# The up projection of a gated feed-forward: high and low activation parts as one 512-column operand

## The chip, the core and the metric

The kernel runs on one core of a Trainium2 chip. Its time is the device time of one execution in microseconds (us), from runs on the chip. TensorE multiplies matrices into PSUM, eight banks of 128 partitions by 512 float32 values; VectorE (DVE), ScalarE (ACT) and GpSimd (POOL) do elementwise work; SyncE (SP) issues the loads of the weights. A profile is one execution taken by the hardware's profiler. In its rows PE is TensorE's matmul, PEld its weight load (the load of the stationary operand, which lies beside the matmul before it).

## The reference, cut to what matters

One decoder layer over 256 tokens of width 2048 in float32. The change lies in the feed-forward part only:

```
def _conv_ffn(h, w_up, conv_w, conv_b, w_down):
    a = h @ w_up                      # (256, 2048) @ (2048, 11264)
    a = depthwise causal convolution of width 3 over the tokens (a) + conv_b
    gate, val = jnp.split(a, 2, axis=-1)
    return (jax.nn.silu(gate) * val) @ w_down
```

The input h of this part is a RMS norm of the residual. Its scale by token is put on after the product, since a product with w_up commutes with it.

## The kernel before

Float32 precision is reached with operands split in two parts of the shorter type float32r: a high part (the value rounded) and a low part (what the rounding lost). A product is three matmuls: high weights by high activations, high weights by low activations, low weights by high activations. The helper `mm3` issues them: for each of 8 row tiles the first two, one behind the other with the same stationary weight tile, and then 8 of the third kind.

The weights come as a stream of chunks of 128 partitions by 1024 values, eight 128x128 tiles each. SP loads a chunk into a `raw` tile (L120), ACT rounds it to `hi` (L150) and DVE takes the difference to `lo` (L151). `w_next` hands out the next split chunk and has the two after it prepared. The pool `wp` has three tiles each of `hi` and `lo`, so a split waits until the chunk three before it has been used by its last matmul.

The up projection is a loop of 44 iterations. Each makes 128 gate channels and 128 value channels for all 256 tokens, out of four chunks: gate first and second half of the 2048 inputs, then value first and second half. Weights are stationary (128x128), activations move (128x256). The activations `x2h` and `x2l` stay in SBUF for the whole loop. Gate and value share one PSUM bank (`mm`, of three), 256 columns each. When both are done, DVE multiplies the bank by the scale by token, `r2`, into `abuf` (L1069); ACT and DVE make the convolution (tile `cv`, L1075 to L1079), ACT the SiLU (L1082), POOL the product (L1083), ACT and POOL the two parts of the result, `hid` (L1084, L1085).

Behind the loop comes the down projection (L1122), with `hid` stationary and `w_down` moving, 512 columns wide: a chunk there is 12 matmuls. At its start DVE transposes the residual `hT` into tiles `ht` (L1100) and ACT issues 16 loads that bring them to `ho` (L1102). These take the place of the activations of the up projection (tags `xh0` to `xh3` and `rA`).

Elsewhere in the kernel one more product has 512 moving columns: the values of the attention (`v_chunk`, L855 to L857), with the latents `chl` stationary and split weights moving.

The order on each engine is set by a scheduler ahead of time; each engine then runs its queue strictly in that order, and waits where an instruction needs another engine's result.

Of the kernel before, what the change touches and what calls it, by code (L numbers as in the profile page):

```python
# [20 lines left out]
# How many steps of the state space follow each chunk of weights until its output is needed: the chunks  # L21
# of u, of the latents, of keys, values and queries, the last heads, the attention half of the output.
# [15 lines left out]
# Column layout of the packed per-partition parameters.  # L38
# [16 lines left out]
def layer_kernel(ctx: ExitStack, tc: tile.TileContext, pack, pos, xt, bk, w_in, w_kpe, w_uqn,  # L55
# [17 lines left out]
    # every chunk: 128 partitions x up to 1024 values, split exactly into two float32r parts  # L73
# [53 lines left out]
    def load_after(dst, src):  # L127
        """A load that stays behind the weights asked for so far."""
        with tc.issue_after(state["last"]):
            SP.dma_start(dst, src)  # L130

    def w_prep_to(n):
        while state["prep"] < min(n, len(chunks)):
# [3 lines left out]
            if i == KPE_AT + 1:  # L137
                # the rotary key is a float32 product with the input rows as they are: its weights take the norm's
# [23 lines left out]
    def mm3(ps, wh, wl, xh, xl, nk, first, last):  # L162
        """ps += sum over k of w[k].T @ x[k], each operand given as two parts."""
# [5 lines left out]

    def col(t, k, n=128):  # L170
        return t[:, k * n:(k + 1) * n]

# [8 lines left out]
    def quads(dtype, name):  # L181
        """Sixteen row tiles, four to a tile."""
# [15 lines left out]
    # the first half of the input rows and of three column tiles arrive two row tiles at a time  # L198
# [27 lines left out]
    # a few products of ones bring the array to its full clock before the data is there  # L226
# [19 lines left out]
    def tok_sums(parts, ps=None):  # L246
        """Sums over partitions and parts, token t of the half h in column h of a PSUM tile."""
# [7 lines left out]
    def tok_rsqrt(ps, n, eps=None):  # L255
        """1 / sqrt(ps / n + eps) by token."""
# [5 lines left out]
    def tok_rows(r):  # L262
        """The values by token as a row, alike in every partition."""
# [6 lines left out]
    def row_scale(dst, parts, n, eps=None):  # L270
        """dst[p, t] = 1 / sqrt(sum over partitions and parts / n + eps), alike in every row."""
        r = tok_rsqrt(tok_sums(parts), n, eps)
        A.copy(dst, tok_rows(r))
        return r

    def split_scaled(hi, lo, src, w):
        """hi + lo = src * w (one value of w per partition), hi in float32r."""
# [26 lines left out]
    def wrap(dst, src, k):  # L304
        """dst = src less the nearest multiple of 2 pi."""
# [14 lines left out]
    # factors of the complex products, the second set for the imaginary part of the other operand  # L320
# [6 lines left out]
    def ssm_setup():  # L327
# [21 lines left out]
        # columns: powers 0..4 of the state layout, then the key layout, each step with its own power  # L349
# [9 lines left out]
        # phase of a chunk of four steps in turns, and in two parts of which one has few bits  # L359
# [24 lines left out]
        # z = (abar - 1) / lambda  # L384
# [18 lines left out]
        # z times the powers, pair index outermost: [re | -im] and [-im | -re]  # L403
# [23 lines left out]
    # cos and sin of i * phi for the 64 chunks, eight pairs at a time  # L427
# [28 lines left out]
    # matrices of the state space, four pairs of groups at a time  # L456
# [8 lines left out]
    def ssm_in_products(b):  # L465
        """Chunk inputs to states times abar, laid [(step, p32), ...]: the two halves of the complex products."""
# [18 lines left out]
    def ssm_out_mats(b, c):  # L485
        """States (times abar) to outputs: C z abar^l, real (c = 0) and negated imaginary part."""
# [40 lines left out]
    def ssm_k(b):  # L527
        """Lag matrices: values of input b against C z abar^l."""
# [11 lines left out]
    def ssm_m(b):  # L540
        """Within a chunk: lag matrices placed by step, the skip on the diagonal."""
# [731 lines left out]
```

## Time and profile before

| | |
|---|---|
| median of 3 runs | 1113.42 us (1112.39 to 1113.47) |
| profiled execution, from first to last instruction | 1111.5 us |
| TensorE busy in it | 1066.4 us, 96% |
| DVE busy | 736.2 us, 66% |
| ACT busy | 611.0 us, 55% |
| POOL busy | 286.0 us, 26% |
| up projection, first to last matmul | 350.4 to 858.2 us |
| mean granted clock of TensorE | 0.991 of 2.4 GHz |

The span of the profiled execution stands 1.9 us below the median of the runs; the rows give no other time of that execution. Busy shares count an engine as busy for the whole modelled duration of its instructions, and matmuls overlap in a pipeline, so the time that one more matmul costs is read from the distance between starts.

### The profile page before, as it was taken

Reading aid. Unit: us, or ns where it says so; the run is one execution under the profiler, and the core shown is the slowest. Engines: PE = TensorE matmul, PEld = TensorE weight load, DVE = VectorE, ACT = ScalarE, POOL = GpSimd, SP = SyncE. Lnnn points to the kernel's source line nnn. Section 1 sums busy time; section 2 is a strip of 40 time slices with the busy share of each in tenths; the row PEclk is TensorE's granted clock in tenths of the full one; section 3 lists DMA queues with packets and bytes.
Section 4 is the critical chain, followed back from the end, with each engine's and each line's share of the span. In section 5 each row is a group of like instructions: output and inputs, shape, how many; then the busy total and the mean of one; then the engine's idle time right before and its main releaser. Section 6 shows DMA issues by size and latency. Waiting matters only on the chain.

```text
span 1111.5 us, 20545 instructions
## 1 busy us (share of the span) xinstructions
PE 1066.4 (96%) x8264; PEld 1002.9 (90%) x8264; DVE 736.2 (66%) x998; ACT 611.0 (55%) x986; POOL 286.0 (26%) x284
## 2 busy tenths in 40 slices
PE   7979899787999999999999999999999999999997
PEld 7979877786999999999999999999999888888896
DVE  8999898797798665656566565665657545454543
ACT  6567578857765645555555455555554434343433
POOL 7371745773333121211212112121211000000000
PEclk9989999999999999999999999999999999999999
DMA  6635341433555455555555555555555965555652
GB/s 211 227 115 172 134 130 61 171 134 131 173 176 186 172 189 189 174 188 180 182 189 183 180 189 174 188 189 180 182 182 185 258 227 189 189 189 189 210 190 76
DMA packets 56672, 195.40 MB, mean 176 GB/s; under 512 B 6528, under 2 KB 8448, under 8 KB 56576
## 3 DMA queue, kind: packets, MB, share of 16 engines
q1 hardware_dynamic: 54576, 190.93, 50.0%
q10 hardware_dynamic: 2000, 3.16, 1.1%
q8 instruction: 65, 1.06, 0.4%
q14 instruction: 31, 0.25, 0.1%
HBM read 189.86 MB, written 2.10 MB: 173 GB/s over the span
## 4 chain that ended last, share of the span: by engine, by line
PE 78%; DVE 11%; ACT 5%; issue 3%; DMA 3%; POOL 0%; SPq 0%; ACTq 0%; DVEq 0%
PE mm L168 18%; PE mm L166 18%; PE mm L165 18%; PE mm L1122 11%; PE wk L1122 11%; DVE lo L151 3%; ACT yT L610 1%; DMA bkt<-in_bk_dram 1%; DVE epad L477 1%; PE wk L913 1%; DVE hT L992 1%; PE wk L912 1%; ACT u L512 1%; DMA raw<-in_w_in_dram 1%; DVE sh L578 1%
## 5 line engine op out<-in xcount | busy, mean ns | idle before, releaser
L151 DVE TENSOR_TENSOR lo<-raw,hi 128x1024 fp32r<-128x1024 f32 x329 | 411.4, 1252 | 256.0 <-ACT hi L150 253.5
L150 ACT CAST hi<-raw 128x1024 fp32r<-128x1024 f32 x329 | 343.4, 1047 | 305.8 <-PE mm L166 113.2
L166 PE MATMUL mm<-x2l,hi 128*128 128x256 f32 x1408 | 345.6, 283 | 0.0
L165 PE MATMUL mm<-x2h,hi 128*128 128x256 f32 x1408 | 345.6, 283 | 0.0
L165 PEld LDWEIGHTS mm<-x2h,hi 128*128 128x128 f32 x1408 | 270.3, 192 | 0.0
L166 PEld LDWEIGHTS mm<-x2l,hi 128*128 128x128 f32 x1408 | 270.3, 192 | 0.0
L168 PE MATMUL mm<-x2h,lo 128*128 128x256 f32 x1408 | 197.6, 283 | 0.0
L168 PEld LDWEIGHTS mm<-x2h,lo 128*128 128x128 f32 x1408 | 181.6, 192 | 0.0
L1083 POOL TENSOR_TENSOR cv<-cv 128x256 f32<-128x256 f32 x44 | 68.0, 1545 | 389.4 <-ACT cv L1082 375.8
L1122 PE MATMUL wk<-hi,hid 128*128 128x512 f32 (+1 forms) x360 | 88.1, 364 | 0.0
L1122 PE MATMUL mm<-hi,hid 128*128 128x512 f32 x312 | 85.4, 395 | 0.0
L1122 PEld LDWEIGHTS wk<-hi,hid 128*128 128x128 f32 x360 | 63.5, 188 | 13.0
L1069 DVE TENSOR_TENSOR abuf<-mm,r 128x512 f32<-128x512 f32 x43 | 29.7, 691 | 62.2 <-PE mm L168 62.2
L1122 PEld LDWEIGHTS mm<-hi,hid 128*128 128x128 f32 x312 | 57.8, 188 | 13.1
L1075 ACT ACTIVATE cv<-abuf,pk 128x256 f32<-128x256 f32 x88 | 48.3, 595 | 28.5 <-DVE abuf L1069 26.9
L1084 ACT CAST hid<-cv 128x256 fp32r<-128x256 f32 x44 | 17.9, 406 | 75.1 <-POOL cv L1083 71.8
L1122 PE MATMUL wk<-lo,hid 128*128 128x512 f32 (+1 forms) x180 | 50.9, 364 | 0.0
L165 PE MATMUL mm<-xh,hi 128*128 128x256 f32 x184 | 48.0, 294 | 2.5 <-ACT hi L150 2.5
L1122 PE MATMUL mm<-lo,hid 128*128 128x512 f32 x156 | 49.0, 395 | 0.0
L166 PE MATMUL mm<-xl,hi 128*128 128x256 f32 x184 | 47.6, 292 | 0.0
L493 POOL TENSOR_TENSOR m<-bkt,pp 128x256 f32<-128x256 f32 x32 | 30.2, 955 | 61.2 <-DMA bkt<-in_bk_dram 47.2
L610 ACT ACTIVATE yT<-wk 32x64 f32<-32x64 f32 x128 | 35.6, 278 | 7.8 <-PE wk L604 6.3
(330 smaller groups left out, 1641.4 us busy)
## 6 DMA issues: line engine op xcount, KB each, us to landing
raw<-in_w_up_dram SPq DMA_DIRECT2D x176, 512.0 KB, 3.2
raw<-in_w_down_dram SPq DMA_DIRECT2D x88, 512.0 KB, 4.2
raw<-in_w_out_dram SPq DMA_DIRECT2D x32, 512.0 KB, 3.3
raw<-in_w_in_dram SPq DMA_DIRECT2D x25, 512.0 KB, 3.3
bkt<-in_bk_dram SPq DMA_DIRECT2D x8, 512.0 KB, 5.6
raw<-in_w_glu_dram SPq DMA_DIRECT2D x8, 512.0 KB, 3.3
raw<-in_w_uqn_dram SPq DMA_DIRECT2D x4, 512.0 KB, 4.3
hT<-in_xt_dram SPq DMA_DIRECT2D x4, 512.0 KB, 4.9
```

What stands on the lines that cost most here:

```text
L150: A.copy(hi, raw)
L151: V.tensor_tensor(out=lo, in0=raw, in1=hi.bitcast(F32), op=ALU.subtract)
L165: PE.matmul(ps, wh(k), xh(k), start=(first and k == 0), stop=False)
L166: PE.matmul(ps, wh(k), xl(k), start=False, stop=False)
L168: PE.matmul(ps, wl(k), xh(k), start=False, stop=(last and k == nk - 1))
L493: G_.tensor_tensor(out=m, in0=ci[:, s].unsqueeze(2).to_broadcast([P, 4, 4, 16]), in1=pp[:, s, c].rearrange("p (q l) -> p q l", l=4)[:, cb, ...
L610: A.activation(dst[:, j], psy[32 * j:32 * j + 32, q], AF.Gelu_apprx_tanh)
L1069: V.tensor_tensor(out=a[:, :, 2:T + 2], in0=ps, in1=r2.unsqueeze(1).to_broadcast([P, 2, T]), op=ALU.mult)
L1075: A.activation(t, a[:, gv, 2:T + 2], AF.Identity, bias=prm("conv_b", ch_, 1), scale=prm("conv_w", 176 + ch_, 1))
L1083: G_.tensor_tensor(out=cv[0], in0=cv[0], in1=cv[1], op=ALU.mult)
L1084: A.copy(hid[0][:, i, :], cv[0])
L1122: PE.matmul(ps[:, 0:n], hid[x][:, 2 * i + k, ts_], w[wk][:, 512 * k + c0:512 * k + c0 + n], start=(i == 0 and s == 0 and k == 0), stop=(i ...
```

## The change

The activations' two parts are laid side by side, `x2(k)` of 2 x 256 columns (tiles `x2a` for the first eight row tiles, `x2b` for the others). A new helper `mm_wide` sends both as one moving operand of 512 columns behind each high weight tile, and the 256 columns of the high part behind each low weight tile. Products with the high activations land in the first half of a bank, products with the low activations and with the low weights in the second half. So gate and value take a bank each, one of the pool `mm` and one of `wk`. On the way out ACT copies the second half to SBUF (`low`), DVE adds the first half to it into `abuf`, and the multiplication by `r2` follows from SBUF to SBUF. Nothing else differs but comments and the numbers of lines (+9 or +10 in this part).

```diff
+    def mm_wide(ps, wh, wl, xp, nk, first, last):
+        n = ps.shape[-1] // 2
+        for k in range(nk):
+            PE.matmul(ps, wh(k), xp(k), start=(first and k == 0), stop=False)
+        for k in range(nk):
+            PE.matmul(ps[:, n:], wl(k), xp(k)[:, 0], start=False, stop=(last and k == nk - 1))
...
-    x2h = r0.tile([P, 16, T], F32R, tag="rA", name="x2h")
-    x2l = quads(F32R, "x2l")
+    x2a = [r0.tile([P, 2, 2, T], F32R, tag=f"xh{i}", name=f"x2{i}") for i in range(4)]
+    x2b = r0.tile([P, 8, 2, T], F32R, tag="rA", name="x2b")
+
+    def x2(k):
+        return x2a[k // 2][:, k % 2] if k < 8 else x2b[:, k - 8]
...
-        split_scaled(x2h[:, ct, :], x2l(ct), hT[:, ct, :], prm("ffn_norm", ct, 1))
+        split_scaled(x2(ct)[:, 0], x2(ct)[:, 1], hT[:, ct, :], prm("ffn_norm", ct, 1))
...
     for i in range(44):
-        if i == 0:
-            pgv = [mm_bank()[:, :T], mm_bank()[:, :T]]
-        else:
-            ps = mm_bank().rearrange("p (a t) -> p a t", a=2)
-            pgv = [ps[:, 0], ps[:, 1]]
+        pgv = [mm_bank(), wk_bank()]
+        a = abuf[i % 2]
         for gv, hf in up_order(i):
             wh, wl = w_next()
-            mm3(pgv[gv], lambda k: col(wh, k), lambda k: col(wl, k),
-                lambda k: x2h[:, 8 * hf + k, :], lambda k: x2l(8 * hf + k), 8, hf == 0, hf == 1)
+            mm_wide(pgv[gv], lambda k: col(wh, k), lambda k: col(wl, k), lambda k: x2(8 * hf + k), 8,
+                    hf == 0, hf == 1)
+            if hf == 1:
+                t = fp.tile([P, T], F32, tag=f"cv{gv}", name="low")
+                A.copy(t, pgv[gv][:, T:])
+                V.tensor_tensor(out=a[:, gv, 2:T + 2], in0=pgv[gv][:, 0:T], in1=t, op=ALU.add)
         if i == 0:
             row_scale(r2, [hacc], D)
-        a = abuf[i % 2]
-        if i == 0:
-            for gv in range(2):
-                V.tensor_tensor(out=a[:, gv, 2:T + 2], in0=pgv[gv], in1=r2, op=ALU.mult)
-        else:
-            V.tensor_tensor(out=a[:, :, 2:T + 2], in0=ps, in1=r2.unsqueeze(1).to_broadcast([P, 2, T]),
-                            op=ALU.mult)
+        V.tensor_tensor(out=a[:, :, 2:T + 2], in0=a[:, :, 2:T + 2], in1=r2.unsqueeze(1).to_broadcast([P, 2, T]),
+                        op=ALU.mult)
```

Where this moves instructions is seen in the order of the built programs, which holds no time. First TensorE's queue, one chunk (second half of a gate) in the middle of the up projection before; a wait names the engine whose counter it watches, and of the eight pairs the first four stand here:

```order
L165 MATMUL mm<-x2h,hi 128x256 [waits Activation_49]
L166 MATMUL mm<-x2l_3725,hi 128x256
L165 MATMUL mm<-x2h,hi 128x256
L166 MATMUL mm<-x2l_3725,hi 128x256
L165 MATMUL mm<-x2h,hi 128x256
L166 MATMUL mm<-x2l_3725,hi 128x256
L165 MATMUL mm<-x2h,hi 128x256
L166 MATMUL mm<-x2l_3725,hi 128x256
```

The same chunk with the change, whole:

```order
L175 MATMUL mm<-x2b,hi 128x512 [waits Activation_49]
L175 MATMUL mm<-x2b,hi 128x512 x7
L177 MATMUL mm<-x2b,lo 128x256 [waits DVE_49]
L177 MATMUL mm<-x2b,lo 128x256 x7
```

A chunk goes from 16 + 8 matmuls of 256 columns to 8 of 512 and 8 of 256. Up to the loop, TensorE's queue is the same in both programs.

Second, ACT's queue in one iteration in the middle of the loop, before (`cv` from `abuf` is the convolution's first term, `hid` the rounded result; DMAHW names the lanes on which loads report):

```order
L150 CAST hi<-raw 128x1024 [waits DMAHW0_49,DVE_49,PE_49]
L1075 ACTIVATE cv<-abuf_4346,pk 128x256 [waits DVE_49]
L1075 ACTIVATE cv<-abuf_4346,pk 128x256
L150 CAST hi<-raw 128x1024 [waits DMAHW1_49,PE_49,Activation_49]
L1082 ACTIVATE cv<-cv 128x256 [waits DVE_49]
L1084 CAST hid_4343<-cv 128x256 [waits Pool_49]
L150 CAST hi<-raw 128x1024 [waits DMAHW2_49,PE_49,Activation_49]
L150 CAST hi<-raw 128x1024 [waits DMAHW3_49,PE_49,Activation_49]
```

And with the change:

```order
L1075 COPY low<-mm 128x256 [waits PE_49,Pool_49]
L1092 ACTIVATE cv<-cv 128x256 [waits DVE_49]
L1094 CAST hid_4343<-cv 128x256 [waits Pool_49]
L150 CAST hi<-raw 128x1024 [waits DMAHW7_49,PE_49,Activation_49]
L150 CAST hi<-raw 128x1024 [waits DMAHW0_49,PE_49,Activation_49]
L1075 COPY low<-wk 128x256 [waits PE_49]
L150 CAST hi<-raw 128x1024 [waits DMAHW1_49,DVE_49,PE_49]
L1085 ACTIVATE cv<-abuf_4346,pk 128x256 [waits DVE_49,Activation_49]
L1085 ACTIVATE cv<-abuf_4346,pk 128x256
L150 CAST hi<-raw 128x1024 [waits DMAHW2_49,PE_49,Activation_49]
```

Two copies have come in, each waiting for TensorE to finish an accumulation, and the SiLU of an iteration now stands behind the copy of the next iteration's gate. The four roundings of weights (L150) stand between them; counted from the start of the loop, the first behind the hid cast belongs to the chunk that TensorE starts three chunks after the gate has ended.

Third, ACT's queue a little behind the loop, where the last loads of `ho` stand between the roundings of the seventh and the eighth chunk of `w_down`, before:

```order
L150 CAST hi<-raw 128x1024 [waits DMAHW5_49,PE_49,Activation_49]
L1102 DMA ho<-ht_10414 32x2x512 [waits DMAHW5_49]
L1090 ACT_TABLE_LOAD
L1090 ACTIVATE warm<-hid_4344,eps_t 128x1 [waits Pool_49]
L1102 DMA ho<-ht_10414 32x2x512 [waits DMAHW6_49]
L1102 DMA ho<-ht_10414 32x2x512 [waits DMAHW7_49]
L1102 DMA ho<-ht_10414 32x2x512 [waits DMAHW1_49]
L150 CAST hi<-raw 128x1024 [waits DVE_49,PE_49] x3
```

And with the change:

```order
L150 CAST hi<-raw 128x1024 [waits PE_49,Activation_49]
L1112 DMA ho<-ht_9312 32x2x512 [waits DMAHW4_49]
L1094 CAST hid_4343<-cv 128x256 [waits Pool_49]
L1112 DMA ho<-ht_9312 32x2x512 [waits DMAHW6_49]
L1112 DMA ho<-ht_9312 32x2x512 [waits DMAHW7_49]
L1100 ACT_TABLE_LOAD
L1100 ACTIVATE warm<-hid_4344,eps_t 128x1 [waits Pool_49]
L1112 DMA ho<-ht_9312 32x2x512 [waits DMAHW1_49]
L150 CAST hi<-raw 128x1024 [waits PE_49,Activation_49]
```

The last `hid` cast has slipped in among the loads, and the loads wait for other lanes; the rounding of the eighth chunk still stands behind the sixteenth load.

## Rows read from the trace of the kernel before

**Rows 1.** The page: busy time by engine, and the chain that ended last.

```profile
PE 1066.4 (96%) x8264; PEld 1002.9 (90%) x8264; DVE 736.2 (66%) x998; ACT 611.0 (55%) x986; POOL 286.0 (26%) x284
PE 78%; DVE 11%; ACT 5%; issue 3%; DMA 3%; POOL 0%; SPq 0%; ACTq 0%; DVEq 0%
PE mm L168 18%; PE mm L166 18%; PE mm L165 18%; PE mm L1122 11%; PE wk L1122 11%; DVE lo L151 3%; ACT yT L610 1%; DMA bkt<-in_bk_dram 1%; DVE epad L477 1%; PE wk L913 1%; DVE hT L992 1%; PE wk L912 1%; ACT u L512 1%; DMA raw<-in_w_in_dram 1%; DVE sh L578 1%
```

**Rows 2.** Windows of 50 us: PE, PEld, DVE, ACT, POOL busy, granted clock, DMA.

```profile
500.00:550.00 50.00, 50.00 (x419) 50.00 (x418) 30.71 (x41) 26.92 (x36) 9.32 (x8) 1.00 0.52 180
600.00:650.00 50.00, 50.00 (x419) 50.00 (x419) 30.39 (x38) 25.11 (x33) 9.04 (x8) 1.00 0.52 184
```

**Rows 3.** Instructions of L165 and L168: durations in ns, first and last start in us.

```profile
L165 PE MATMUL mm<-x2h,hi x1408: 279/283/362, 350.4 to 857.0; 128*128 128x256 f32 x176
...
L168 PE MATMUL mm<-x2h,lo x1408: 281/283/283, 352.3 to 858.0; 128*128 128x256 f32 x176
```

**Rows 4.** Timeline of PE in the up projection: start, us, instruction.

```profile
600.77 0.28 PE L166 MATMUL mm<-x2l,hi 128*128 128x256 f32 x1
600.89 1.12 PE L168 MATMUL mm<-x2h,lo 128*128 128x256 f32 x8
601.85 0.28 PE L165 MATMUL mm<-x2h,hi 128*128 128x256 f32 x1
601.97 0.28 PE L166 MATMUL mm<-x2l,hi 128*128 128x256 f32 x1
...
603.77 1.12 PE L168 MATMUL mm<-x2h,lo 128*128 128x256 f32 x8
604.73 0.28 PE L165 MATMUL mm<-x2h,hi 128*128 128x256 f32 x1
```

**Rows 5.** The chain in order of time, in the down projection: six 512-column matmuls a piece.

```profile
978.73 1.40 PE mm L1122 x6
```

**Rows 6.** Timeline of PE at the first chunk of attention values (512 columns).

```profile
155.07 0.40 PE L855 MATMUL mm<-hi,chl 128*128 128x512 f32 x1
...
155.54 0.39 PE L857 MATMUL mm<-lo,chl 128*128 128x512 f32 x1
...
156.46 0.39 PE L855 MATMUL mm<-hi,chl 128*128 128x512 f32 x1
...
156.91 0.39 PE L857 MATMUL mm<-lo,chl 128*128 128x512 f32 x1
...
157.59 0.39 PE L857 MATMUL mm<-lo,chl 128*128 128x512 f32 x1
```

**Rows 7.** Timeline of PE in the last quarter of the down projection: 256 columns.

```profile
1089.97 1.53 PE L1122 MATMUL wk<-xw,hid 128*128 128x256 f32 x12
1091.33 1.09 PE L1122 MATMUL mm<-hi,hid 128*128 128x512 f32 x4
```

**Rows 8.** Groups by line and form: count, busy us, mean ns, idle before.

```profile
L273 ACT COPY r<-wk 128x256 f32<-128x256 f32 x1 | 0.4, 372 | 1.2 <-PE wk L266 1.2
L1067 DVE TENSOR_TENSOR abuf<-mm,r 128x256 f32<-128x256 f32 x2 | 0.8, 420 | 0.3 <-ACT r L273 0.3
L1132 DVE TENSOR_TENSOR ho<-ho,fw 128x512 f32<-128x512 f32 x6 | 3.9, 684 | 0.0
L1069 DVE TENSOR_TENSOR abuf<-mm,r 128x512 f32<-128x512 f32 x43 | 29.7, 691 | 62.2 <-PE mm L168 62.2
```

**Rows 9.** Timeline of ACT over one iteration: start, us, idle before and its releaser.

```profile
651.73 1.10 ACT L1075 ACTIVATE cv<-abuf,pk 128x256 f32<-128x256 f32 x2 [0.64 <-DVE abuf L1069]
652.97 1.05 ACT L150 CAST hi<-raw 128x1024 fp32r<-128x1024 f32 x1
654.05 0.42 ACT L1082 ACTIVATE cv<-cv 128x256 f32<-128x256 f32 x1
656.18 0.41 ACT L1084 CAST hid<-cv 128x256 fp32r<-128x256 f32 x1 [1.71 <-POOL cv L1083]
656.49 1.04 ACT L150 CAST hi<-raw 128x1024 fp32r<-128x1024 f32 x1
```

**Rows 10.** Timeline behind the loop: PE's start of the down projection; ACT and PE at its eighth chunk.

```profile
858.16 1.10 PE L1122 MATMUL mm<-hi,hid 128*128 128x512 f32 x4
...
875.54 0.59 ACTq L1102 DMA_DIRECT2D ho<-ht  x1
...
876.23 2.95 ACT L150 CAST hi<-raw 128x1024 fp32r<-128x1024 f32 x3 [2.14 <-DMA raw<-in_w_down_dram]
...
877.77 1.10 PE L1122 MATMUL mm<-hi,hid 128*128 128x512 f32 x4
```

## Prediction

> **What bounds the kernel now.** I read the page first. TensorE is busy for 96% of the span, and 78% of the chain that ended last is its work; the three lines of `mm3` alone (L165, L166, L168) hold 18% each [rows 1]. A busy share of an engine whose matmuls overlap proves little, so the second view is the windows. In the up projection TensorE shows no hole in 50 us, at the full clock (granted share 1.00, the 2.4 GHz level), with DVE at 30.4 to 30.7 us and ACT at 25 to 27 us of the 50 [rows 2]. DVE and ACT can't be the bound there; TensorE is, and what a change does to its pace is worth its whole amount.
>
> The pace is read from starts, not from durations. Two neighbouring matmuls of 256 columns start at 601.85 and 601.97, eight of the third kind take from 600.89 to 601.85, and a whole chunk of 24 takes from 600.89 to 603.77, 2.88 us [rows 4]: 120.0 ns each. The stage bears it out. There are 1408 matmuls on each of the three lines, 4224 in all [rows 3], and 4224 x 0.1200 = 506.9 us, against 507.8 us from the first start, 350.4 [rows 3], to the first matmul of the down projection at 858.16 [rows 10]. The 0.9 us left over are the two row sums and their like at the first iteration. So there is no wait in this stage to be won or lost; there is only the pace.
>
> **What the change does to TensorE.** 1408 pairs of 256-column matmuls with one weight tile become 1408 matmuls of 512 columns; the 1408 on L168 stay as they are, at 120.0 ns. A pair costs 240.0 ns now. The question is what one of 512 columns costs in its place, and the up projection has no such row. Two other places have.
>
> In the down projection six of them take 1.40 us [rows 5]: 233.3 ns each. There weights move and `hid` is stationary. In the attention's values the latents are stationary and weights move, and the run starts right behind 256-column matmuls of the same `mm3` that the up projection has. Its first eight take from 155.07 to 156.91, 1.84 us or 230.0 ns each; the later ones settle lower, from 156.46 to 157.59 five of them, 226.0 ns each [rows 6]. All three are float32r, 128 stationary columns, full clock.
>
> The bounds are then:
> - 226.0 ns: 14.0 ns less than a pair, x 1408 = 19.7 us gained.
> - 233.3 ns: 6.7 ns less, 9.4 us gained.
>
> I take 230.0 ns. The new stream is eight of 512 behind eight of 256, again and again, and the eight first rows of the values are just that, behind 256-column matmuls that also run at 120 ns. The down projection's 256-column matmuls run at another pace, twelve from 1089.97 to 1091.33 or 113.3 ns [rows 7], so whatever sets the pace there differs. The gain is 10.0 ns x 1408 = 14.1 us; a chunk goes from 2.88 to 2.80 us.
>
> The Trainium skill (TensorE: Matmul & The Clock Gate, Back-to-back issue gap) gives the distance between two matmuls as the columns at 2.4 GHz and about 2.5 ns more, 109 ns for 256 columns and 216 ns for 512. By that a pair in one saves only the 2.5 ns, 3.5 us in all, an estimate from that page, and the time would be 1109.9 us. The trace has 120.0 and 226 to 233 ns, both higher, so the rows decide here; but it warns that the gain hangs on a small remainder.
>
> **What the change does elsewhere.** Gate and value each get a copy of 128x256 from PSUM on ACT, 0.37 us, and an add of 128x256 on DVE, 0.42 us; the multiplication of 512 columns moves from PSUM to SBUF, 0.69 us before, 0.68 us by the nearest row [rows 8]. ACT gets 88 x 0.37 = 33 us, DVE 88 x 0.42 = 37 us, over a stage of 494 us. That is 3.3 and 3.7 us in 50, on top of 27 and 31 us [rows 2]. I cost both at nothing: they lie beside TensorE.
>
> What could break that cover is the order, since ACT rounds the weights too. The copy of the gate waits for TensorE's last matmul of the accumulation, and SiLU, the `hid` cast and two roundings are queued behind it. From the gate's end to the first of these roundings done: copy 0.37 us [rows 8], SiLU 0.42, the wait for POOL's product 1.71, `hid` cast 0.41, rounding 1.05 [rows 9], about 4.0 us. The chunk it is for starts three chunks later, 8.4 us after the gate's end. So 4.4 us are left, and DVE's difference behind it is needed only when the eight wide matmuls of that chunk are through. Were the cover gone, each us of lag beyond 4.4 would stop TensorE for as long in each of 44 iterations.
>
> The other resources: an iteration took one bank of three, and now takes one of three and one of five; a bank is asked for again three iterations on, over 30 us after its add. `low` shares the slots of `cv`; its copy waits for POOL to be done with an earlier `cv`, which it is some 5 us into an iteration of 11.2 us. The stream of weights runs 3% faster at a DMA share of 0.52 [rows 2]. None of these costs.
>
> **Behind the loop** one place is tight already. ACT's queue holds 16 loads of `ho` between the roundings. The rounding of the eighth chunk of `w_down` starts at 876.23, behind the sixteenth load at 875.54, and ends 1.05 us later, at 877.28; TensorE takes it up at 877.77 [rows 10]. The margin is 0.5 us. With the change one more copy and two more adds stand ahead, DVE has all eight transposes in one piece, and the loads wait for other lanes. The cost is bounded by nothing and by the 2.1 us that ACT stood there [rows 10]; the queue has as many loads as before, so I take 0.4 us, once.
>
> **The sum**: -14.1 + 0.4 = -13.7 us. The profiled span of 1111.5 us becomes 1097.8 us. It lies 1.9 us below the median of the runs, and I keep that distance: 1113.4 - 13.7 = 1099.7 us.
>
> **Rivals.**
> 1. *Small gain.* Each chunk switches back from 256 to 512 columns, and the first two wide matmuls behind such a switch take 155.07 to 155.54, 235 ns each [rows 6]. If all eight went like these, the gain would be 5 ns x 1408 = 7.0 us: 1106.8 us with the 0.4. Against it: the next six of the same run are faster. The page named above would put the time a little higher still.
> 2. *No gain.* A wide matmul could cost just two narrow ones, 240.0 ns, if each 256 columns of these activations carry their own 13 ns over the 106.7 ns that 256 columns need at 2.4 GHz. Nothing is then saved: 1113.8 us. No row has 512 columns at 240.
> 3. *Slower.* In the last quarter of the down projection two narrow matmuls cost 226.7 ns and a wide one 233.3 [rows 5, 7]: there width costs 2.9%. The same ratio on the pair of 240.0 ns gives 247 ns, and 7 ns x 1408 = 9.9 us lost: 1123.7 us. It decides from 240 ns on. For it speaks that these are the only rows with both widths of one kind side by side; against it that the wide ones cost 233.3 at most in either place, in runs of hundreds, and that it is the narrow ones that differ, 113.3 against 120.0.
> 4. *ACT as the bound*, by the lag worked out above. It needs 4.4 us more of lag in each iteration, and the rows show ACT idle for nearly half of the stage. I count it into the slower case.
>
> **How the numbers follow.** 226.0 to 233.3 ns, the forecast: 0.75, with its own range of 1094 to 1104.4 us. Small gain: 0.12. No gain: 0.06. Slower: 0.07. A measurement of this kernel can tell about 0.2% or 2.2 us from no change, so faster is 0.75 + 0.12 = 0.87, same 0.06, slower 0.07. The range starts at the lower bound, 1113.4 - 19.7 = 1093.7 us, and goes up to take in the small gain, 1107.5 us; it leaves out about 2 in 10.
>
> **What would show it.** In the profile after, the starts of wide matmuls should stand 226 to 233 ns apart (the mean of a chunk's first eight), the narrow ones 120 ns, a chunk 2.80 us, the loop some 494 us, with TensorE without holes in the windows. ACT should show 88 copies of 0.37 us, DVE 88 adds of 0.42 us, and the waits of the weights' roundings should still end on TensorE and not the other way round. A hole of TensorE of up to 2 us some 20 us behind the loop would be the tight place. The prediction is wrong if the wide ones stand 236 ns or more apart, if the narrow ones change their pace, or if TensorE waits for a rounding in each iteration.

## The result and the profile after

| | before | after |
|---|---|---|
| time, median of 4 runs | 1113.24 us (1112.39 to 1113.47) | 1098.03 us (1096.98 to 1098.56) |
| ratio, with its 95% interval | 1 | 0.9862 (0.9849 to 0.9874) |
| span of the profiled execution | 1111.5 us | 1096.4 us |
| up projection, first matmul to the first of the down projection | 507.8 us | 492.5 us |

The change made the kernel 15.2 us faster; 13.7 us had been forecast. The up projection alone gives back 15.3 us. These are the windows of the changed kernel, with the columns of [rows 2]:

```profile
500.00:550.00 50.00, 50.00 (x289) 44.02 (x288) 35.75 (x51) 28.74 (x47) 8.95 (x10) 1.00 0.64 190
600.00:650.00 50.00, 50.00 (x288) 43.97 (x287) 35.87 (x52) 28.74 (x47) 8.83 (x9) 1.00 0.64 190
```

TensorE still has no hole, and the clock is the same. What is new stands in the second number: the weight loads (PEld) filled all 50 us before [rows 2], and now 44. That is a sign of wider spacing and no more: in the up projection a load's record is 187 to 193 ns long with few exceptions, in every kernel here, so loads that start closer together than that fill the span. DVE and ACT work 5 and 2 to 4 us more in 50 and still wait for TensorE.

Two chunks from the timeline of TensorE (start, us, instruction), and the end of the loop:

```profile
602.09 1.12 PE L177 MATMUL mm<-x2b,lo 128*128 128x256 f32 x8
603.04 2.00 PE L175 MATMUL wk<-x,hi 128*128 128x512 f32 x8
604.88 1.12 PE L177 MATMUL wk<-x,lo 128*128 128x256 f32 x8
...
843.26 1.10 PE L1132 MATMUL mm<-hi,hid 128*128 128x512 f32 x4
```

Read starts, not durations: eight wide ones take from 603.04 to 604.88, 1.84 us or 230.0 ns each; the eight narrow ones behind them 0.95 us, 119 ns each. A chunk is 2.79 us, where it was 2.88 [rows 4]. Over all 1408 of each kind the single starts give 230.1 and 119.1 ns. Within a run of eight the wide ones stand 233.3, 235.8, 228.3, 232.5 and 230.8 ns apart and then three times 226.7 (the settled pitch from here on); the first narrow one behind them has 113.3, the second 119.2, the others 120.0.

The groups of the added work (line, form, count, busy us, mean ns, idle before):

```profile
L1075 ACT COPY low<-mm 128x256 f32<-128x256 f32 x44 | 16.4, 372 | 0.0
L1075 ACT COPY low<-wk 128x256 f32<-128x256 f32 x44 | 16.1, 366 | 0.0
L1076 DVE TENSOR_TENSOR abuf<-mm,low 128x256 f32<-128x256 f32 x44 | 18.4, 418 | 0.0
L1076 DVE TENSOR_TENSOR abuf<-wk,low 128x256 f32<-128x256 f32 x44 | 18.4, 417 | 0.0
L1079 DVE TENSOR_TENSOR abuf<-abuf,r 128x512 f32<-128x512 f32 x44 | 30.4, 692 | 1.4
```

The waits of 400 to 800 us (who waits, for whom, us, times, the longest) show ACT's roundings waiting for the wide matmuls, not these for ACT; no row there has TensorE waiting:

```profile
ACT hi L150 <- PE mm L175: 50.1, 35, 1.4
ACT hi L150 <- issue: 49.4, 40, 1.3
ACT hid L1094 <- POOL cv L1093: 46.3, 36, 1.3
```

And the tight place behind the loop [rows 10], from the timeline of ACT:

```profile
861.76 2.94 ACT L150 CAST hi<-raw 128x1024 fp32r<-128x1024 f32 x3
```

And from that of TensorE:

```profile
862.87 1.17 PE L1132 MATMUL mm<-hi,hid 128*128 128x512 f32 x4
863.87 1.10 PE L1132 MATMUL wk<-hi,hid 128*128 128x512 f32 x4
```

The first of the three roundings, at 1.05 us [rows 9], ends at 862.81; TensorE starts on its tile at 862.87, and four wide ones take 1.00 us there where four at 233.3 take 0.93. The margin of half a microsecond is gone, and less than 0.1 us is lost. From the first matmul of the down projection to the end it is 253.1 us, where it was 253.4.

### The profile page after: what moved, and what is told of

Same layout as the page of the kernel before. It is cut to its first block, busy times and chain, and to the rows that moved or that the text cites. A ratio compares the mean times of both kernels' runs of the same rounds, so it can differ in the third digit from the quotient of the medians.

```text
span 1096.4 us, 18029 instructions
## 1 busy us (share of the span) xinstructions
PE 1053.3 (96%) x6856; PEld 930.4 (85%) x6856; DVE 771.4 (70%) x1085; ACT 626.7 (57%) x1074; POOL 269.6 (25%) x284
## 4 chain that ended last, share of the span: by engine, by line
PE 78%; DVE 10%; ACT 6%; issue 3%; DMA 3%; POOL 0%; ACTq 0%; SPq 0%; DVEq 0%
PE mm L175 15%; PE wk L175 15%; PE mm L1132 11%; PE wk L1132 11%; PE wk L177 8%; PE mm L177 8%; PE mm L168 3%; PE mm L166 3%; PE mm L165 3%; DVE lo L151 2%; ACT yT L619 2%; DMA raw<-in_w_in_dram 1%; ACT hi L150 1%; DVE epad L486 1%; PE wk L922 1%
## 5 line engine op out<-in xcount | busy, mean ns | idle before, releaser
L150 ACT CAST hi<-raw 128x1024 fp32r<-128x1024 f32 x329 | 343.8, 1048 | 320.4 <-PE wk L1132 113.3
L175 PE MATMUL mm<-x2b,hi 128*128 128x512 f32 x352 | 88.3, 392 | 0.0
L175 PE MATMUL wk<-x2b,hi 128*128 128x512 f32 x352 | 88.3, 392 | 0.0
L175 PE MATMUL mm<-x,hi 128*128 128x512 f32 x352 | 88.2, 392 | 0.0
L175 PE MATMUL wk<-x,hi 128*128 128x512 f32 x352 | 88.1, 392 | 0.0
L175 PEld LDWEIGHTS wk<-x2b,hi 128*128 128x128 f32 x352 | 63.4, 189 | 11.3
L175 PEld LDWEIGHTS mm<-x,hi 128*128 128x128 f32 x352 | 63.3, 189 | 11.3
L175 PEld LDWEIGHTS mm<-x2b,hi 128*128 128x128 f32 x352 | 63.3, 189 | 11.3
L175 PEld LDWEIGHTS wk<-x,hi 128*128 128x128 f32 x352 | 63.3, 189 | 11.3
L177 PEld LDWEIGHTS mm<-x2b,lo 128*128 128x128 f32 x352 | 48.1, 190 | 3.4
L177 PEld LDWEIGHTS wk<-x,lo 128*128 128x128 f32 x352 | 48.0, 190 | 3.4
L165 PE MATMUL mm<-xh,hi 128*128 128x256 f32 x184 | 47.9, 294 | 2.5 <-ACT hi L150 2.5
```

What stands on the lines that cost most here:

```text
L150: A.copy(hi, raw)
L165: PE.matmul(ps, wh(k), xh(k), start=(first and k == 0), stop=False)
L175: PE.matmul(ps, wh(k), xp(k), start=(first and k == 0), stop=False)
L177: PE.matmul(ps[:, n:], wl(k), xp(k)[:, 0], start=False, stop=(last and k == nk - 1))
```

## The experiments

Theory: what a matmul costs beyond its columns is paid once for 512 columns and twice for two times 256; the copies, adds and banks of the change cost nothing. Rivals: the gain comes from the layout in PSUM; or from reading one contiguous piece; or the surplus belongs to where operands lie, and not to the width. A pitch is the distance from the start of one matmul to the start of the next; those below are means over the loop from single starts. Each ratio is to the kernel before in the same session.

```
kernel          wide ns   narrow ns     loop us   time us    ratio to before (95%)
before             -        120.0        507.8    1113.24    1
after            230.1      119.1        492.5    1098.03    0.9862 (0.9849-0.9874)
two_narrow         -        120.0        507.8    1113.70    1.0002 (0.9993-1.0012)
strided          230.1      119.1        492.5    1099.36    0.9873 (0.9857-0.9888)
alternate        236.3      117.1        498.2    1104.84    0.9927 (0.9912-0.9942)
snake            228.6        119.5      490.8    1097.33    0.9851 (0.9837-0.9864)
quarter          238.0   108.5 (of 128)  641.4    1247.07    1.1204 (1.1178-1.1230)
before_pad64       -        117.8        498.0    1103.83    0.9918 (0.9903-0.9932)
after_pad64      232.8      114.1        489.2    1094.57    0.9831 (0.9815-0.9848)
after_pad32      232.8      119.0        496.0    1101.77    0.9897 (0.9882-0.9911)
probe_before       -     see its text    500.7    1105.18    0.9922 (0.9904-0.9940)
probe_after    see its text              495.6    1099.71    0.9873 (0.9854-0.9892)
mix              229.8      117.8        490.1    1094.83    0.9841 (0.9826-0.9856)
snake_pad64      233.1      113.7        489.1    1095.12    0.9838 (0.9823-0.9852)
```

**two_narrow: the change without its width.**

```diff
-            PE.matmul(ps, wh(k), xp(k), start=(first and k == 0), stop=False)
+            PE.matmul(ps[:, :n], wh(k), xp(k)[:, 0], start=(first and k == 0), stop=False)
+            PE.matmul(ps[:, n:], wh(k), xp(k)[:, 1], start=False, stop=False)
```

> The layout of the change stays (both parts of a row tile side by side, two banks for an iteration, the low half copied by ACT and added by DVE), but each 512-column matmul is issued as two of 256 columns into the two halves of the bank. Theory (the gain is the width of the matmul alone): all matmuls of the loop are 120 ns again, 2816 of them in place of 1408 of 230.14 ns, 1408 x (240.0 - 230.1) = 13.9 us back: 1112 us, ratio to the kernel before 0.998 to 1.001. Rival (the gain comes from the layout: the three products no longer pile up on one and the same 256 columns of PSUM): the time stays at 1098 us, ratio 0.986. If the copies and adds cost something that the width hides, it shows as a time above 1114 us.

Its timeline of TensorE has 120 ns everywhere:

```profile
603.27 0.28 PE L175 MATMUL wk<-x2b,hi 128*128 128x256 f32 x1
603.39 0.28 PE L176 MATMUL wk<-x2b,hi 128*128 128x256 f32 x1
603.51 0.28 PE L175 MATMUL wk<-x2b,hi 128*128 128x256 f32 x1
```

And its windows have the weight loads at 50 us of 50 again:

```profile
500.00:550.00 50.00, 50.00 (x419) 50.00 (x419) 33.70 (x46) 27.13 (x43) 7.80 (x9) 1.00 0.56 185
```

The loop takes 507.8 us, as before, with the copies, adds and banks of the change in it. So the layout gives nothing and the copies and adds cost nothing; the width, which means one matmul and one weight load fewer for each pair, is the whole gain.

**strided: two pieces of 256 columns in one matmul.**

```diff
-    x2b = r0.tile([P, 8, 2, T], F32R, tag="rA", name="x2b")
+    x2b = r0.tile([P, 2, 8, T], F32R, tag="rA", name="x2b")
...
-        return x2a[k // 2][:, k % 2] if k < 8 else x2b[:, k - 8]
+        return x2a[k // 2][:, :, k % 2] if k < 8 else x2b[:, :, k - 8]
```

> The wide matmul stays, but its 512 columns are two pieces of 256 columns that do not lie side by side in SBUF. Theory (what is paid once for each instruction is saved, whatever the addresses are): wide ones 230 ns apart, 1098 us, ratio 0.986. Rival (the surplus belongs to each contiguous piece that is read, so one operand must be one piece): wide ones 236 to 240 ns apart, 8 to 14 us more, 1106 to 1112 us.

The loop is 492.5 us, the same to the last tenth, and the pitches by place in the run are the same too. One contiguous piece is not needed. Its time is 1.3 us above the changed kernel's, within the two intervals; in the profiled execution 0.9 us was one longer wait of TensorE at the tight place behind the loop.

**alternate and snake: shorter and longer runs.** The first puts both matmuls into one loop over k:

```diff
             PE.matmul(ps, wh(k), xp(k), start=(first and k == 0), stop=False)
-        for k in range(nk):
             PE.matmul(ps[:, n:], wl(k), xp(k)[:, 0], start=False, stop=(last and k == nk - 1))
```

> Wide and narrow matmuls alternate (high weight tile, then low weight tile of the same k) in place of eight wide and then eight narrow. In the changed kernel the first five wide ones behind a narrow one are 228 to 236 ns, the later three 226.7; the first two narrow ones behind a wide one are 113 to 115 ns, the later six 120. Theory A (each switch from narrow to wide costs): every wide one is 233 to 236 ns and every narrow one 114, 347 to 350 ns a pair against 349.3 now: 1095 to 1099 us. Theory B (a narrow matmul is 120 ns because the next weight tile is not in place sooner, and behind a wide one it is): 226.7 + 113.3 = 340 ns a pair, 9.2 ns x 1408 = 13 us less: 1085 us. Theory C (run length does not matter, each kind has its own price): 349.3 ns, 1098 us.

```profile
602.14 0.40 PE L175 MATMUL mm<-x,hi 128*128 128x512 f32 x1
602.37 0.28 PE L176 MATMUL mm<-x,lo 128*128 128x256 f32 x1
602.49 0.40 PE L175 MATMUL mm<-x,hi 128*128 128x512 f32 x1
...
604.96 0.40 PE L175 MATMUL mm<-x2b,hi 128*128 128x512 f32 x1
```

From 602.14 to 604.96 there are eight pairs, 352.5 ns each; over the loop a wide one is 236.3 and a narrow one 117.1 ns, 353.4 against 349.3. The loop is 5.7 us longer. Theory B was wrong by a wide margin: a narrow one behind a wide one is a little cheaper, and the wide one behind it dearer by more. Theory A was near with the wide one, 236.3 for its 233 to 236, but took the narrow one at 114 instead of 117.1, so its 347 to 350 ns was too low. Theory C, no difference, fails as well.

The second turns the order round in every other chunk, so that runs of 16 meet:

```diff
-        for k in range(nk):
-            PE.matmul(ps, wh(k), xp(k), start=(first and k == 0), stop=False)
-        for k in range(nk):
-            PE.matmul(ps[:, n:], wl(k), xp(k)[:, 0], start=False, stop=(last and k == nk - 1))
+        for k in range(nk):
+            if not last:
+                PE.matmul(ps, wh(k), xp(k), start=(first and k == 0), stop=False)
+            else:
+                PE.matmul(ps[:, n:], wl(k), xp(k)[:, 0], start=False, stop=False)
+        for k in range(nk):
+            if not last:
+                PE.matmul(ps[:, n:], wl(k), xp(k)[:, 0], start=False, stop=False)
+            else:
+                PE.matmul(ps, wh(k), xp(k), start=False, stop=(k == nk - 1))
```

> The second half's chunk of an accumulation does its eight narrow matmuls ahead of its eight wide ones, so that runs are of 16 and not of 8; the number of each is the same. Alternating them cost 4 ns a pair (353.3 against 349.3). In the changed kernel the eight wide ones of a chunk take 27.5 ns more than 8 x 226.7, and the narrow ones 7 ns less than 8 x 120. Theory (this is paid once for each switch): 88 switches fewer x 20.5 ns = 1.8 us less, 1096.2 us, the sixth to sixteenth wide one of a run at 226.7 ns. Rival (it depends on the place in the chunk, the first five tiles of a high part): 1098.0 us and the same numbers by place as now.

```profile
601.57 2.00 PE L183 MATMUL mm<-x2b,hi 128*128 128x512 f32 x8
603.41 1.98 PE L176 MATMUL wk<-x,hi 128*128 128x512 f32 x8
605.22 1.12 PE L181 MATMUL wk<-x,lo 128*128 128x256 f32 x8
```

The first eight of a run take 1.84 us, the second eight 1.81: the dear first five are a matter of the switch, as the theory had it, and the loop is 1.6 us shorter. But the time is only 0.7 us lower, within the intervals. About as much was lost behind the loop, where ACT now stands in the loads of `ho`, and TensorE behind the roundings; 23 wide matmuls from 861.21 to 867.28 take 6.07 us, where 23 at 233.3 ns take 5.37. The timeline of ACT:

```profile
860.84 0.41 ACT L1100 CAST hid<-cv 128x256 fp32r<-128x256 f32 x1 [1.86 <-DMA ho<-ht]
...
864.36 2.96 ACT L150 CAST hi<-raw 128x1024 fp32r<-128x1024 f32 x3
```

And that of TensorE:

```profile
861.21 0.86 PE L1138 MATMUL wk<-hi,hid 128*128 128x512 f32 x3
...
867.28 0.40 PE L1138 MATMUL wk<-hi,hid 128*128 128x512 f32 x1
```

**quarter: the other way, 128 columns.**

```diff
-            PE.matmul(ps[:, n:], wl(k), xp(k)[:, 0], start=False, stop=(last and k == nk - 1))
+            PE.matmul(ps[:, n:n + 128], wl(k), xp(k)[:, 0, 0:128], start=False, stop=False)
+            PE.matmul(ps[:, n + 128:], wl(k), xp(k)[:, 0, 128:256], start=False, stop=(last and k == nk - 1))
```

> In the changed kernel each narrow matmul (256 columns) on a low weight tile becomes two of 128 columns, each with its own load of the same weight tile. Theory F (a matmul costs its columns at 2.4 GHz, and a fixed surplus of 13.3 ns): 53.3 + 13.3 = 66.7 ns each, 133.3 ns in place of 119.1, 1408 x 14.2 = 20 us more, 1118 us. Theory L (the pace of a short matmul is a floor that its weight load sets, and 256 columns just reach it): 113 to 120 ns each, 235 in place of 119, 1408 x 117 = 165 us more, 1263 us; the merging then saves a whole weight load where two stood, and no width below 256 columns is worth anything.

This run says what sets the pace below 256 columns. Its timeline, from the last wide ones of a chunk:

```profile
602.10 0.62 PE L175 MATMUL mm<-x2b,hi 128*128 128x512 f32 x2
602.56 0.22 PE L177 MATMUL mm<-x2b,lo 128*128 128x128 f32 x1
602.62 0.27 PE L178 MATMUL mm<-x2b,lo 128*128 128x128 f32 x1
602.73 0.28 PE L177 MATMUL mm<-x2b,lo 128*128 128x128 f32 x1
...
603.74 0.28 PE L178 MATMUL mm<-x2b,lo 128*128 128x128 f32 x1
```

The first narrow one is followed after 0.06 us, about what 128 columns need. The ten behind it take from 602.62 to 603.74, 112 ns each, although they have half the columns of those at 119. A fixed surplus of 13.3 ns alone (theory F) would have given 66.7. The quick one saves nothing either: the first wide one behind a run has 283 ns in the mean, some 50 more than the others. The timeline of the weight loads shows why:

```profile
602.33 0.19 PEld L177 LDWEIGHTS mm<-x2b,lo 128*128 128x128 f32 x1
602.56 0.19 PEld L178 LDWEIGHTS mm<-x2b,lo 128*128 128x128 f32 x1
602.67 0.19 PEld L177 LDWEIGHTS mm<-x2b,lo 128*128 128x128 f32 x1
602.78 0.19 PEld L178 LDWEIGHTS mm<-x2b,lo 128*128 128x128 f32 x1
```

The loads start 0.11 us apart from 602.56 on, also where the matmuls have 0.06, and from 400 to 800 us no two of them start less than 108 ns apart; within a run most have 111 or 112. So there is a floor of 108 to 112 ns for a matmul with weights of its own, and it is the load's. Whether it also sets the pace at 256 columns is not shown: in the kernel before, loads start 120 ns apart, 8 ns or more above the floor, each 3 ns behind the start of a matmul.

**Where operands lie.** In the built program the weight parts and the activations all start at byte 96 of a 128-byte line, and `hid`, stationary in the down projection, at byte 32. Padding ahead of the weights moves everything on that side of SBUF, the tiles that the weights are loaded into and `hid` included, so a run with padding doesn't say which tile counts:

```diff
+    pad = ctx.enter_context(tc.tile_pool(name="pad", bufs=1)).tile([P, 16], F32, name="pad")
     wp = ctx.enter_context(tc.tile_pool(name="wp", bufs=3))
...
+    V.memset(pad, 0.0)
```

> The kernel before with 64 bytes of padding ahead of the weight tiles, so that all weights and hid lie 64 bytes later against the activations; nothing else differs but one small memset. Theory (120 against 113.3 ns of a 256-column matmul comes from where the stationary and the moving operand lie): 256-column matmuls with weights stationary go to 113.3 ns, 4224 x 6.7 = 28 us in the loop and some 12 us in the stages ahead, 1073 to 1085 us; those of the down projection may go to 120 ns. Rival (placement plays no part, it is what the array does between two matmuls): 1113 us, ratio 1.000.

The kernel before gets 9 us faster by 64 bytes. In its timeline of TensorE the runs on the low parts of two neighbouring chunks start 2.83 us apart, 24 matmuls of 117.9 ns; the loop's mean is 117.8, not the 113.3 of the theory:

```profile
601.05 1.10 PE L169 MATMUL mm<-x2h,lo 128*128 128x256 f32 x8
603.88 1.10 PE L169 MATMUL mm<-x2h,lo 128*128 128x256 f32 x8
```

In the down projection, where `hid` has moved to byte 96, the narrow ones went from 113.8 to 118.1 ns in the mean, and the wide ones stayed at 233.2. So the place plays a part, in either direction, but the number that the theory gave it was too large.

In the probes every weight tile is 32 bytes longer than what is used, so the three buffers lie at three places:

```diff
-                    hi = wp.tile([P, 1024], F32R, tag="hi", name="hi")
-                    lo = wp.tile([P, 1024], F32R, tag="lo", name="lo")
+                    hi = wp.tile([P, 1032], F32R, tag="hi", name="hi")[:, 0:1024]
+                    lo = wp.tile([P, 1032], F32R, tag="lo", name="lo")[:, 0:1024]
```

> The kernel before, with each tile of weights 32 bytes longer than what is used of it, so that the three buffers of a part start at three places: high parts at byte 96, 0 and 32 of a 128-byte line, low parts at 64, 96 and 0; the activations stay at byte 96. One run so shows every place, each chunk of weights at its own pace. With 64 bytes of padding the 256-column matmul had gone from 120.0 to 117.8 ns. Theory P1 (what counts is whether the stationary tile starts on a 64-byte boundary): the eight low-part matmuls go at 113.3 ns from the buffers at 0 and 64, at 120 from the one at 96. Theory P2 (what counts is the distance between stationary and moving operand): 120 at 96, 117.8 at 32, and 0 and 64 alike, anywhere between 113.3 and 120. Rival P3 (the pace is set by the stretch of the program and not by the single buffer): all chunks at one pace.

Low parts at byte 64, 96 and 0: 118.9, 117.8 and 119.4 ns in the mean, each irregular within its run of eight. High parts at 96, 0 and 32: 119.7, 118.5 and 116.4. Byte 96, 120.0 in the kernel before, is not 120.0 here, and byte 32, 117.8 with the padding, has 116.4. None of P1, P2 and P3 describes that.

> The same three places of the weight buffers in the changed kernel. If the surplus of the narrow matmul goes with the place, the surplus of the wide one (now 226.7 to 235.8 ns, 230.1 in the mean) should go with it: 220 to 227 ns at a place where the narrow one has 113.3, and the transition from narrow to wide (233, 236, 228, 233, 231 ns for the first five) should get shorter. If the wide one is 230 at every place, placement is a matter of the weight loads of short matmuls alone, and the gain of the change would shrink where the place is good: 2 x 113.3 = 226.7 ns for a pair, no gain left.

Wide ones at byte 96, 0 and 32: 230.0, 234.4 and 232.5 ns; narrow ones at 64, 96 and 0: 117.5, 120.5 and 119.7. The surplus of a wide one does not go with that of a narrow one.

> The changed kernel with the 64 bytes of padding that took the kernel before from 120.0 to 117.8 ns a narrow matmul (9 us faster). Theory (a wide one saves the surplus of one narrow one, whatever its size): two narrow ones are 235.6 ns there, so a wide one at 230 saves 5.6 ns x 1408 = 8 us and the narrow ones at 117.8 give 1.3 x 1408 = 1.9 us: 1095 to 1097 us, 7 to 9 us below the padded kernel before. Rival (placement and width are independent savings): 1098.0 - 9 = 1089 us. Rival (at this place the wide one is the same price as two narrow ones, 235.6 ns): 1104 us, no gain from the change at all.

```profile
602.41 1.07 PE L178 MATMUL mm<-x2b,lo 128*128 128x256 f32 x8
603.32 2.02 PE L176 MATMUL wk<-x,hi 128*128 128x512 f32 x8
605.18 1.07 PE L178 MATMUL wk<-x,lo 128*128 128x256 f32 x8
```

Eight narrow ones in 0.91 us, 113.8 ns each; eight wide ones in 1.86, 232.5 each. Single starts give 226 ns for the first wide one and then 236 and 231 in turn: with the weights at byte 32 the up projection has the two prices of the down projection [rows 5, 7]. The loop is 3.3 us shorter than the changed kernel's. The change is worth 9.3 us at this place (1103.83 to 1094.57) and 15.2 at the old one. The two savings do not add up to the rival's 1089, and a pair is not the same price as a wide one either. The time lies just below the first theory's 1095 to 1097, but that is luck: it had the wide one at 230 ns and the narrow one at 117.8, and they are 232.8 and 114.1. The wide one saves only 2.8 ns of the pair's 235.6, and the narrow one behind it gives 3.7.

> The changed kernel with 32 bytes of padding: weights start on a 128-byte line, activations stay at byte 96. The buffer at byte 0 in the probe had wide ones at 234.4 and narrow ones at 119.5 ns; if a buffer's place decides by itself, all chunks are like that: 353.9 ns a pair against 349.3, 6.5 us more, 1104.5 us. If the mixture of three places made that pace in the probe, a uniform place can be as good as the unpadded one: 1098 us.

351.8 ns a pair, 3.7 us above the changed kernel: between the two answers, so it decides neither.

Last, the two best prices together, with the low parts in a pool of their own behind 64 bytes of padding (and 64 behind it, which leaves `hid` at its byte):

```diff
+    pad0 = ctx.enter_context(tc.tile_pool(name="pad0", bufs=1)).tile([P, 16], F32, name="pad0")
+    wlp = ctx.enter_context(tc.tile_pool(name="wlp", bufs=3))
...
-                    lo = wp.tile([P, 1024], F32R, tag="lo", name="lo")
+                    lo = wlp.tile([P, 1024], F32R, tag="lo", name="lo")
```

> The changed kernel with the high weight parts left at byte 96 of a 128-byte line, where the wide matmuls settle at 226.7 ns and have 230.1 in the mean, and only the low parts moved to byte 32, where the narrow ones are 113.3 to 114.1 ns (hid stays at its byte 32). If each kind takes the pace of its own place: 230.1 + 114.1 = 344.2 ns a pair against 349.3 now and 346.9 with all weights moved, 1408 x 5.1 = 7 us less: 1091 us, the fastest of all. Rival (what counts is the common place of the two parts, since a weight load runs beside the matmul of the tile ahead of it): the wide ones lose what the narrow ones gain, as in the probe with three places: 348 to 354 ns a pair, 1096 to 1105 us.

```profile
601.06 2.00 PE L178 MATMUL wk<-x,hi 128*128 128x512 f32 x8
602.90 1.11 PE L180 MATMUL wk<-x,lo 128*128 128x256 f32 x8
603.84 2.00 PE L178 MATMUL wk<-x2b,hi 128*128 128x512 f32 x8
```

The wide ones keep their 229.8 ns, but the narrow ones get to 117.8, not to 114.1. Of the hoped 5.1 ns a pair 1.7 came, so neither answer holds: the wide ones go by their own place, and the narrow ones don't go by theirs alone.

The down projection of this run shows one thing more. There `hid` lies 128 bytes later, so at the same byte of a line, and the tiles `xw`, which hold some of the weights, did not move at all. Yet the narrow matmuls of `xw` by `hid` went from 113.7 to 117.7 ns in the mean. The byte within a 128-byte line, the measure that all these theories used, does not name a place fully.

> Runs of 16 and the 64 bytes of padding together. In the unpadded kernel the runs of 16 made the loop 1.6 us shorter (490.9 against 492.5) and lost 1.3 us behind it, where TensorE waits for roundings behind the last loads of the residual. If both add up: 0.3 to 1.6 us below the changed kernel with padding alone; if the padded place has no dear switch from narrow to wide, no difference.

Nothing was added: 1095.12 us against 1094.57. The loop is 489.1 us, 489.2 without the longer runs: with all weights at byte 32 there are no dear first five, so longer runs have nothing to save.

The fastest measured are after_pad64, mix and snake_pad64, at 1094.6 to 1095.1 us. They are about 3 us below the changed kernel by their medians; the interval of after_pad64 lies just outside that of the changed kernel, those of the other two overlap it at the edge.

## Why the prediction was right

- **The bound.** TensorE's pace set the stage, before and after: no hole in the windows, and a loop that is 1408 x (230.1 + 119.1) = 491.7 us of its 492.5. This step was right.
- **The wide price.** 230.0 ns was taken from the first eight of the attention's values [rows 6], and 230.1 was measured: 13.9 us for 14.1. The reason given, wide behind narrow, holds. The starts between those of [rows 6] are

```profile
155.31 0.40 PE L856 MATMUL mm<-hi,chl 128*128 128x512 f32 x1
155.77 0.40 PE L855 MATMUL mm<-hi,chl 128*128 128x512 f32 x1
156.00 0.39 PE L856 MATMUL mm<-hi,chl 128*128 128x512 f32 x1
156.24 0.39 PE L857 MATMUL mm<-lo,chl 128*128 128x512 f32 x1
```

  and give, from single starts, 234, 236, 228, 232, 231 ns and then 226 to 227: place by place the steps of the new stream. In snake the second eight settle at 226.7. But it was also luck of the place, which the prediction didn't look at: in both products both operands start at byte 96 of a line. With the weights 64 bytes on, a wide one has 232.8 in the mean, and the settled ones 231 and 236 in turn, which is the down projection's 233.3. So the bounds, 226.0 and 233.3, are two prices of the same matmul, and padding alone turned the one into the other.
- **The narrow price** was the term that was mis-sized, if only a little. It was left at 120.0 and was 119.1, since the first one behind a run of wide ones has 113.3: 1408 x 0.9 = 1.2 us more gain, most of the 1.5 us by which the forecast fell short. The prediction had named any change of the narrow pace as a sign of being wrong; this one is small, but it was not foreseen.
- **Copies, adds, banks at nothing.** Right, and shown: two_narrow has them all and takes 507.8 us for its loop, as before. They were 0.37 and 0.42 us, as taken.
- **Behind the loop** 0.4 us was taken; less than 0.1 was lost at the place named. The margin that the step worked with is used up, as snake and strided show, which lose 0.7 to 0.9 us there, and probe_after, where two starts stand 2.24 us apart there, 2.0 more than a wide one takes: about the 2.1 us that the step had as its upper bound.
- **No gain, and slower.** Two_narrow and the pitches rule both out for this kernel. The slower rival paired the prices of the down projection's last quarter, 233.3 and 113.3. Both do occur in the up projection, in after_pad64. But a stream of nothing but narrow ones does not hold 113.3 at that place: before_pad64 has 117.8, so a pair there is 235.6 and the wide one still wins. Why the same matmul is cheaper in runs of eight between wide ones isn't settled.
- **Small gain.** The wide ones aren't all like the first two: 233.3, 235.8, and 226.7 from the sixth on.

What the prediction left open is what kind of remainder is saved. At this place it is one amount for each matmul, whatever its width: at the granted 2.4 GHz 256 columns take 106.7 ns and 512 take 213.3, and the settled pitches are 120.0 and 226.7, 13.3 ns more in either case. A pair in one saves that once; the dear first five take back 27.5 ns in eight, 3.4 for each, and the narrow one gives 0.9. That is 10.8 ns x 1408 = 15.2 us, and the loop got 15.3 us shorter. It is a fit to one place and not a rule: 64 bytes on, narrow ones have 113.4 to 117.8 and wide ones 231 to 236. Nor is it shown whether the 13.3 ns belong to the matmul or to its weight load, since each matmul here has a load of its own; two narrow ones behind one load were not run.

Quarter adds a floor under this, 108 to 112 ns for each load, so that matmuls of 128 columns save next to nothing over 256. It lies below the 120.0 of the kernel before and doesn't explain the gain. The Trainium skill (TensorE: Matmul & The Clock Gate, LDWEIGHTS (loading the stationary operand)) says that a load takes its columns at 1.2 GHz; for 128 columns that is 106.7 ns, an estimate from that page. The trace of quarter agrees, within 5%: 112 ns. The Trainium skill (same page, Back-to-back issue gap) says that in a stream of loads and matmuls the spacing is set by both. The trace agrees in that the loads set it with 128 columns and do not with 512. The formula from that section that the prediction weighed, columns at 2.4 GHz and 2.5 ns, is given there for an isolated matmul, which the prediction didn't say. By it a wide one would have 216 ns, an estimate, where the lowest settled pitch here is 226.7.

Still open: what the 13.3 ns are, why a narrow one has 113, 118 or 120 and a wide one 226 to 236, and by which rule places matter. The probes and mix show that a buffer's own place doesn't decide alone.

## What to carry to other kernels

In a loop without a hole on TensorE, read the distance between starts and set it beside what the columns take at the granted clock: 120.0 and 106.7 ns here. The difference was paid once for each matmul, so two operands that share a weight tile could go as one. Splitting goes the other way: with 128 columns the loads set the pace, and two halves cost 225 ns where one matmul had cost 119. The busy share of the weight loads doesn't tell which case it is: it is 50 of 50 in the kernel before, and 45 in quarter, whose loads do set the pace of two matmuls in three. Take the price of the merged form from the row whose neighbours, and whose operands' places, are most like the new ones. Before comparing two forms of a loop that only TensorE bounds, try one or two paddings of each: here 64 bytes were worth 9 us to one form and 3.5 to the other.

## What was not expected of the hardware

- A 256-column matmul of the up projection took 120.0 ns, or 117.8 when all that lies on the weights' side of SBUF had moved by 64 bytes, and 113.4 there in runs of eight between wide ones. With `hid` moved by 128 bytes, the narrow ones of `xw` took 117.7 for 113.7.
- The switch from narrow to wide costs five dear matmuls (27.5 ns in all) with all weights at byte 96 and none at byte 32.
- GpSimd's product `cv` got shorter, though nothing in it was changed. Its group in 400 to 800 us, after; in the kernel before the same group had a mean of 1582 ns. No run looked into it; it is off the path.

```profile
L1093 POOL TENSOR_TENSOR cv<-cv 128x256 f32<-128x256 f32 x36 | 42.3, 1176 | 314.6 <-ACT cv L1092 314.6
```
